# A mixture-of-experts gather that reads a reordered copy of its rows, in a four-part fused kernel

## The chip, the cores and the metric

The kernel runs on one core of a Trainium2 chip as one launch. The metric is the device time of one execution in microseconds, as the median over runs. TensorE (PE, with its weight loads shown apart as PEld), VectorE (DVE), ScalarE (ACT), GpSimd (POOL) and SyncE (SP) are the engines named below. SP does nothing here but issue weight loads, and GpSimd issues the small loads.

## The reference

Two layers of a transformer block (four kinds of attention, a cross attention over a memory, and a mixture of experts) are followed by four layers of a second block (pooling, neighbourhood attention, convolution, pooling) on 256 rows of width 1024, all in float32. What matters here is the mixture of experts of the first block:

```python
def hierarchical_moe(x, w_group, b_group, w_expert, b_expert, w_gate, w_up, w_down):
    ...
    hid = jax.nn.silu(jnp.einsum('sd,edf->sef', xs, w_gate)) * jnp.einsum('sd,edf->sef', xs, w_up)
    return jnp.einsum('sef,efd->sd', hid * gates[:, :, None], w_down)
```

Each of the 256 rows picks one of 8 groups of experts and two of the four experts in it, so each expert sees only the few rows that chose it. The hidden width of an expert is 256, and an expert's three matrices are 1 MB each.

## The kernel before

The stage `moe` (from line 1477) runs once in each of the two layers. It takes the 32 experts as 8 quads `q` of four. The router (line 1307) gives every row its rank within each expert. Each expert has 32 slots in a pass, so a quad has 128 slots. A one-hot matrix `disp` (line 1388, or a piece of the `y` tiles in the first quad and in extra passes) says which row goes into which slot.

`gather` multiplies: the stationary operand (`lhsT`, loaded as weights) is a 128-column piece of `x`, the moving operand is the one-hot matrix of 128 columns, and the result is the chosen rows, transposed, for one eighth of the width. There are 8 pieces and two blocks of 128 rows, so 16 matmuls for a gather. A float32 matmul appears in the trace as two records of each kind, so a gather is 32 PE records. The pieces are `self.x[tb][:, k0 + j::8]`: every eighth column, since the expert weights are loaded with `(p k)` rows.

After the gather come the gate and up products with 32 columns of weights (`gate_up`, `ps<-w,xg`), the down products (`down`, `ps<-w,y`) and the scatter back into four accumulators (`acc<-y,ct`). The order on PE is: gate and up of quad q, gather of quad q+1, the small transposes of `combine_mats` and `down_in`, down of quad q. In between run pieces of other work that the stage carries along, marked `pl`: the memory's keys and values in layer 0, and the pooling of the second block's context in layer 1.

An expert with more than 32 rows needs more passes. `mores[q]` is the number of passes of a quad, held in a register of every engine. Behind `tc.If(more > 1)` stands a first extra pass, inside it behind `tc.If(more > 2)` a second, unrolled too, and inside that behind `tc.If(more > 3)` a loop for the rest. This stands twice for each quad, in the up part (lines 1533 to 1541) and in the down part (lines 1584 to 1591). All engines run through these branches; the hint of `mark_branch_hint_location` is given for PE alone. A loop of this kind is compiled with a close in which every engine waits for the work and the loads issued ahead of it.

The weights come through rings of 1 MB buffers, filled by SP in the order of use. A load is issued when its buffer is free, so SP waits for PE.

Ahead of the router's scores stands the affine step of the layer norm (`ln_affine`, lines 1098 to 1105), on the four halves of `x`: two on GpSimd, two on DVE, a multiplication and an addition each. At the end of the stage four operations on DVE (line 1608) add the accumulators to the scaled `x`, half by half.

Of the kernel before, what the change touches and what calls it, by code (L numbers as in the profile page):

```python
# [14 lines left out]
OP = mybir.AluOpType  # L15
AX = mybir.AxisListType

P = 128
# [5 lines left out]
ALPHA = 4.0 ** 0.25  # L24
# [111 lines left out]
class Net:  # L136
# [958 lines left out]

        self.flow.spawn(gen(), 0)

    def ln_affine(self, rows, eng=None):

        for tb in range(2):  # L1100
            for nh in range(2):
                e = eng[2 * tb + nh] if eng else self.nc.gpsimd
                x = self.x[tb][:, nh * 512:nh * 512 + 512]
                e.tensor_tensor(x, x, rows[0][nh], OP.mult)
                e.tensor_tensor(x, x, rows[1][nh], OP.add)

    def trans_bank(self, xs, j):

# [197 lines left out]
    def router(self, l, wr, rb):  # L1306

        nc = self.nc
        xf = [self.M2("xf32") for _ in range(4)]
        yield 0, 4.0  # L1310
        for j in range(4):
            self.affine_t(xf[j], self.trans_bank(self.halves(self.x), j), j,
                          lambda k: self.col("ln_mem_g", 8 * l + k), lambda k: self.col("ln_mem_b", 8 * l + k))
            yield 0.6, 0
        self.ln_affine(self.rows, (nc.gpsimd, nc.gpsimd, nc.vector, nc.vector))
        yield 0, 0.8
        p = self.ps()
        for tb in range(2):
# [25 lines left out]
        p = self.ps()  # L1344
# [47 lines left out]
    def gather(self, d, xg):  # L1392

        res = []
        dv = d.rearrange("p t e s -> p t (e s)")
        for k0 in range(0, 8, 4):
            p = self.ps()
            for j in range(4):
                for tb in range(2):
                    self.mm(p[:, j * P:(j + 1) * P], self.x[tb][:, k0 + j::8], dv[:, tb, :], tb == 0 and j == 0, tb == 1)  # L1400
            t = xg[k0 // 4].rearrange("p (k s) -> p k s", k=4)
            if k0:
                self.nc.vector.tensor_copy(xg[1], p)  # L1403
            else:
                self.nc.scalar.copy(xg[0], p)
            res += [t[:, j, :] for j in range(4)]
        return res
# [68 lines left out]
    def moe(self, l):  # L1476
        nc, tc = self.nc, self.tc
# [7 lines left out]
        hx = self.e("hx", [P, EXTRA * 256])  # L1485
# [3 lines left out]
        h, h2 = self.places()  # L1489
# [11 lines left out]
        def between(n):  # L1501

            if l == 0:
                if n in MEM_AT:
                    self._ahead()
                    yield from self.piece(side[0])
            elif n in (3, 6, 7):
                yield from self.piece(side[0])
            elif 10 <= n <= 21:
                self._ahead()  # L1510
                yield from self.piece(side[1])

        for q in range(8):
            if q == 1 and l == 0:
                prep = self.flow.spawn(self.band(), 0)
            wg = [self.raw("E", "expert_w_gate", l, 4 * q + j, 8) for j in range(4)]
            wu = [self.raw("E", "expert_w_up", l, 4 * q + j, 8) for j in range(4)]
            gv, uv = [w for w, _ in wg], [w for w, _ in wu]
            more = mores[q]
            rk = self.s("rk", [P, 2, 4], bufs=1)  # L1520
            if q:
                h, h2 = self.places()

            def extra_up(out):
                nc.vector.tensor_scalar(rk, rk, -32.0, None, OP.add)
                self.gate_up(self.gather(self.dispatch(rk, onehot(h2)), [self.y(0), self.y(1)]), gv, uv, out)

            gates = gates or rest()
            now, d0 = comb, d
            if q < 7:  # L1530
                d = self.dispatch(rank[:, :, 4 * q + 4:4 * q + 8])
            self.gate_up(xg, gv, uv, h)
            with tc.If(more > 1, label=f"up{l}_{q}"):  # L1533
                nc.vector.tensor_copy(rk, rank[:, :, 4 * q:4 * q + 4])
                extra_up(hx[:, 0:256])
                with tc.If(more > 2):
                    extra_up(hx[:, 256:512])
                    with tc.If(more > 3):
                        with tc.For_i(3, more) as i:
                            extra_up(h2)  # L1540
                            nc.vector.tensor_copy(hx[:, self.at(i)], h2)
            tc.mark_branch_hint_location(f"down{l}_{q}", more > 1, pe)
            for _, i in wg + wu:
                self.used(i)
            if q == 3:
                self.far.close()
                if l:
                    self.near.close()
                    assert self.plan is None or not self.live_p
                self.other(split=SPLITS, more=MORE[l])  # L1550
                if l:
                    self.perm, self.capp = self.near.enter_context(self.tc.tile_pool(name="late", bufs=LATE, reuse_waits="tile", side="right")), LATE
                self.keep, self.stage = True, 2 * l + 1
                self.n_split = SPLITS
                self.pump()
                main.lane = "ps"
            yield 8.5, 0
            yield from between(3 * q)
            if q < 7:
                xg = self.gather(d, xt)  # L1560
                now = now or self.combine_mats(flat(d0), gates[:, :, 0, :])
                comb = self.combine_mats(flat(d), gates[:, :, q + 1, :])
                ht = self.down_in(h)
                yield 5.0, 0 if q > 2 else 3.0
                yield from between(3 * q + 1)
            else:
                ht = self.down_in(h)
            if q == 7 and not l:
                self.adas.append(self.flow.spawn(self.ada(1), 2, 6.0))
            gq = gates[:, :, q, :]  # L1570
            wd = [self.raw("E", "expert_w_down", l, 4 * q + j, 2) for j in range(4)]
            dv = [w for w, _ in wd]

            def extra_down(h, src=None):
                dx, h2 = self.places()
                if h is None:
                    h = h2
                    nc.vector.tensor_copy(h, src)
                nc.vector.tensor_scalar(rk, rk, -32.0, None, OP.add)
                d2 = self.dispatch(rk, onehot(dx))  # L1580
                self.down(self.down_in(h), dv, *self.combine_mats(flat(d2), gq, "x"))

            def extras():
                with tc.If(more > 1, label=f"down{l}_{q}"):
                    nc.vector.tensor_copy(rk, rank[:, :, 4 * q:4 * q + 4])
                    extra_down(hx[:, 0:256])
                    with tc.If(more > 2):
                        extra_down(hx[:, 256:512])
                        with tc.If(more > 3):
                            with tc.For_i(3, more) as i:  # L1590
                                extra_down(None, hx[:, self.at(i)])

            self.down(ht, dv, *now, q == 0)
            extras()
            if q < 7:
                tc.mark_branch_hint_location(f"up{l}_{q + 1}", mores[q + 1] > 1, pe)
            if q == 7:
                nc.scalar.preload_act_table_set("natural_log_exp_and_others")
            for _, i in wd:
                self.used(i)  # L1600
            if q == 7:
                self._ahead()
            if q == 7:
                st = [self.s("bn", [P, 2, 6], bufs=2) for _ in range(2)]
                for half in range(2):
                    for tb in range(2):
                        x = self.x[tb][:, half * 512:half * 512 + 512]
                        nc.vector.scalar_tensor_tensor(x, x, ALPHA, self.acc[tb][half], OP.mult, OP.add)
                        self.bn_half(st, half, tb)
            yield 6.0, 0 if q > 2 else 10.0  # L1610
            yield from between(3 * q + 2)
            if q == 2 and l == 0:
                yield prep.done
# [530 lines left out]
    def layer_b(self, l):  # L2144

        with ExitStack() as ctx:
            self.phase(ctx, 6)
            self.stage = 2 * l
            self.other(ring2=RING2)
            self.exp = ctx.enter_context(self.tc.tile_pool(name="exp", bufs=1, reuse_waits="tile"))  # L2150
            self.y = lambda i, dt=F32: self.e(f"y{i}", [P, 512], dt)
            self.rows = [[], []]
            for i in range(4):
                t, c = self.y(i), i % 2 * 512
                self.nc.sync.dma_start(t, self.a["ln_mem" + ("_g", "_b")[i // 2]][l:l + 1, c:c + 512].to_broadcast([P, 512]))
                self.rows[i // 2].append(t)
            self.wr = self.router_weights(l)
            self.pump()
            yield from self.moe(l)

# [188 lines left out]
```

## Time and profile before

| | us |
|---|---|
| median of 3 runs | 1836.73 (1834.0 to 1844.76) |
| the profiled execution | 1837.78 |
| its span, first to last instruction | 1836.0 |
| stage `moe`, layer 0 (gather of quad 0 to the last scatter) | 306 to 602 |
| stage `moe`, layer 1 | 876 to 1250 |

The profiled execution lies 1.05 us above the median and has 1.8 us outside its span. [...] Further views read the trace of one stretch: the waits of an engine with the one that released it, the windows with busy times and granted clock, and the timeline of an engine.

### The profile page before, as it was taken

The page shows a single profiled execution, that of the slowest core. Times are in us where ns is not written, and L with a number is a line of the kernel's source. Part 1 is how long each engine was busy: PE and PEld are TensorE (multiplying, and loading weights), DVE is VectorE, ACT ScalarE, POOL GpSimd, SP SyncE. Part 2 cuts the span into 40 slices and gives each one's busy share as a digit, 9 for nine tenths or more (in the row PEclk, how much of TensorE's full clock was granted, in tenths as well). Part 3 has the DMA queues.
Part 4 walks back from the last instruction along what each step waited for, and adds up shares of the span by engine and source line. Part 5 has one row for each costly group of instructions (what it writes and reads, how often), then busy time and mean ns, then how long its engine had stood idle before and what let it go on. Part 6 is the DMA issues. An engine that isn't in the chain of part 4 may idle for free. (4 is left out here: it accounts for less than half of the span.)

```text
span 1836.0 us, 29061 instructions
## 1 busy us (share of the span) xinstructions
PE 1649.1 (90%) x11357; PEld 1297.9 (71%) x11357; DVE 918.4 (50%) x2160; ACT 701.1 (38%) x1422; POOL 165.9 (9%) x248
## 2 busy tenths in 40 slices
PE   7999997788888799988898898997998999899997
PEld 6767985556765466686656675866887886699785
DVE  5567545252112756766121243247555566576645
ACT  4654540102212355442010132234545565455543
POOL 4000201000000300031000000002001112000101
PEclk9999998899999899999899999998998999999999
DMA  8266557989957955576357497897456866385630
GB/s 306 85 204 229 187 206 302 389 327 416 364 197 310 385 164 183 184 285 255 129 223 329 168 412 301 317 364 280 139 188 135 207 97 84 121 293 171 235 111 24
DMA packets 145964, 427.29 MB, mean 233 GB/s; under 512 B 12252, under 2 KB 19652, under 8 KB 121172
## 3 DMA queue, kind: packets, MB, share of 16 engines
q1 hardware_dynamic: 140660, 411.19, 60.6%
q0 software_dynamic: 5088, 13.32, 5.3%
q8 instruction: 124, 2.03, 0.5%
q14 instruction: 92, 0.75, 0.1%
HBM read 423.43 MB, written 1.05 MB: 231 GB/s over the span
## 5 line engine op out<-in xcount | busy, mean ns | idle before, releaser
L308 DVE TENSOR_TENSOR wlo<-w,whi 128x512 fp32r<-128x512 f32 (+2 forms) x586 | 395.4, 709 | 265.0 <-ACT whi L307 262.8
L307 ACT CAST whi<-w 128x512 fp32r<-128x512 f32 (+2 forms) x592 | 341.5, 611 | 249.6 <-PE ps L366 199.1
L366 PE MATMUL ps<-xth,whi 128*128 128x256 f32 x896 | 263.9, 295 | 8.7 <-ACT whi L307 5.2
L366 PE MATMUL ps<-xth,wlo 128*128 128x256 f32 x896 | 259.3, 289 | 4.4 <-DVE wlo L308 4.4
L366 PE MATMUL ps<-xtl,whi 128*128 128x256 f32 x896 | 258.5, 289 | 0.6 <-DVE xtl L1142 0.4
L366 PE MATMUL ps<-whi,xth 128*128 128x512 f32 (+2 forms) x512 | 206.6, 404 | 4.4 <-ACT whi L307 4.0
L366 PE MATMUL ps<-wlo,xth 128*128 128x512 f32 (+2 forms) x512 | 198.8, 388 | 0.2 <-DVE wlo L308 0.2
L366 PE MATMUL ps<-whi,xtl 128*128 128x512 f32 (+2 forms) x512 | 198.6, 388 | 0.2 <-DVE xtl L1142 0.2
L366 PEld LDWEIGHTS ps<-xth,whi 128*128 128x128 f32 x896 | 176.0, 196 | 18.1 <-ACT whi L307 12.8
L366 PEld LDWEIGHTS ps<-xth,wlo 128*128 128x128 f32 x896 | 174.8, 195 | 5.2 <-DVE wlo L308 5.2
L366 PEld LDWEIGHTS ps<-xtl,whi 128*128 128x128 f32 x896 | 175.2, 196 | 3.2 <-issue 1.4
L366 PEld LDWEIGHTS ps<-whi,xth 128*128 128x128 f32 x512 | 99.0, 193 | 33.2 <-ACT whi L307 6.6
L366 PEld LDWEIGHTS ps<-whi,xtl 128*128 128x128 f32 x512 | 98.4, 192 | 20.7 <-DVE xtl L1142 0.9
L366 PEld LDWEIGHTS ps<-wlo,xth 128*128 128x128 f32 x512 | 98.9, 193 | 18.3 <-DVE wlo L308 1.3
L366 PE MATMUL ps<-disp,x 128*128 128x128 f32 x384 | 94.4, 414 | 15.7 <-PEq L1533 6.8
L366 PEld LDWEIGHTS ps<-disp,x 128*128 128x128 f32 x384 | 93.0, 336 | 19.0 <-issue 14.3
L366 PE MATMUL ps<-w,xg 128*32 128x256 f32 x1536 | 86.9, 382 | 6.1 <-issue 2.8
L366 PE MATMUL ps<-w,y 128*32 128x512 f32 (+1 forms) x784 | 80.9, 551 | 6.9 <-DVE y L1451 4.4
L366 PEld LDWEIGHTS ps<-w,xg 128*32 128x32 f32 x1536 | 52.1, 111 | 40.2 <-issue 7.3
L1142 POOL TENSOR_TENSOR xtl<-aff,xth 128x512 fp32r<-128x512 f32 x9 | 11.6, 1285 | 696.9 <-ACT xth L1141 521.5
L1403 DVE COPY xg<-ps 128x512 f32<-128x512 f32 x14 | 9.7, 692 | 118.9 <-PE ps L366 118.9
L1435 DVE TENSOR_TENSOR y<-y,ps 128x256 f32<-128x256 f32 x12 | 5.1, 421 | 112.6 <-ACTq L1533 62.9
(516 smaller groups left out, 2567.0 us busy)
## 6 DMA issues: line engine op xcount, KB each, us to landing
w<-in_expert_w_gate_dram SPq DMA_DIRECT2D x64, 1024.0 KB, 14.4
w<-in_expert_w_up_dram SPq DMA_DIRECT2D x64, 1024.0 KB, 12.6
w<-in_expert_w_down_dram SPq DMA_DIRECT2D x64, 1024.0 KB, 10.0
w<-in_ada_w_dram SPq DMA_DIRECT2D x48, 1024.0 KB, 6.1
w<-in_pool_w_in_dram SPq DMA_DIRECT2D x24, 1024.0 KB, 10.9
w<-in_na_w_in_dram SPq DMA_DIRECT2D x24, 1024.0 KB, 6.5
w<-in_w_in_dram SPq DMA_DIRECT2D x16, 1024.0 KB, 11.5
w<-in_conv_w_in_dram SPq DMA_DIRECT2D x16, 1024.0 KB, 6.0
```

The source lines that it names most:

```text
L307: self.nc.scalar.copy(hi, src)
L308: (self.nc.gpsimd if self.spare and k % 2 else self.nc.vector).tensor_tensor(lo, src, hi.bitcast(F32), OP.subtract)
L366: self.nc.tensor.matmul(out, lhsT, rhs, start=start, stop=stop, skip_group_check=True)
L1142: (nc.gpsimd if j == 2 else nc.vector).tensor_tensor(lo, fs[j - 1], hi.bitcast(F32), OP.subtract)
L1403: self.nc.vector.tensor_copy(xg[1], p)
L1435: nc.vector.tensor_tensor(h, sg, p[:, 256:512], OP.mult)
```

## The change

The addition of `ln_affine` ahead of the router writes its result to a new pair of tiles `xp`, of shape 128 x 8 x 128, in which column `8 j + k` of `x` stands at `[k, j]`. `gather` reads the 128-column piece `xp[tb][:, k0 + j, :]`, which is unbroken. At the end of the stage line 1608 reads `xp` in place of `x`, through the same reordering, and writes `x` in natural order.

In the extra code the second, unrolled pass goes, and the loop runs from 2 in place of 3, in the up part and in the down part.

The SBUF kept for the descriptors of GpSimd's DMAs is set to 8192 bytes of a partition, where it was 16384; the two new tiles take 8192 bytes.

```diff
--- before.py
+++ after.py
@@ -1095,14 +1095,18 @@
 
         self.flow.spawn(gen(), 0)
 
-    def ln_affine(self, rows, eng=None):
+    def ln_affine(self, rows, eng=None, xp=None):
 
         for tb in range(2):
             for nh in range(2):
                 e = eng[2 * tb + nh] if eng else self.nc.gpsimd
                 x = self.x[tb][:, nh * 512:nh * 512 + 512]
                 e.tensor_tensor(x, x, rows[0][nh], OP.mult)
-                e.tensor_tensor(x, x, rows[1][nh], OP.add)
+                o, b = x, rows[1][nh]
+                if xp:
+                    o = xp[tb].rearrange("p k j -> p j k")[:, nh * 64:nh * 64 + 64, :]
+                    x, b = (v.rearrange("p (j k) -> p j k", k=8) for v in (x, b))
+                e.tensor_tensor(o, x, b, OP.add)
 
     def trans_bank(self, xs, j):
 
@@ -1312,7 +1316,7 @@
             self.affine_t(xf[j], self.trans_bank(self.halves(self.x), j), j,
                           lambda k: self.col("ln_mem_g", 8 * l + k), lambda k: self.col("ln_mem_b", 8 * l + k))
             yield 0.6, 0
-        self.ln_affine(self.rows, (nc.gpsimd, nc.gpsimd, nc.vector, nc.vector))
+        self.ln_affine(self.rows, (nc.gpsimd, nc.gpsimd, nc.vector, nc.vector), self.xp)
         yield 0, 0.8
         p = self.ps()
         for tb in range(2):
@@ -1397,7 +1401,7 @@
             p = self.ps()
             for j in range(4):
                 for tb in range(2):
-                    self.mm(p[:, j * P:(j + 1) * P], self.x[tb][:, k0 + j::8], dv[:, tb, :], tb == 0 and j == 0, tb == 1)
+                    self.mm(p[:, j * P:(j + 1) * P], self.xp[tb][:, k0 + j, :], dv[:, tb, :], tb == 0 and j == 0, tb == 1)
             t = xg[k0 // 4].rearrange("p (k s) -> p k s", k=4)
             if k0:
                 self.nc.vector.tensor_copy(xg[1], p)
@@ -1534,11 +1538,9 @@
                 nc.vector.tensor_copy(rk, rank[:, :, 4 * q:4 * q + 4])
                 extra_up(hx[:, 0:256])
                 with tc.If(more > 2):
-                    extra_up(hx[:, 256:512])
-                    with tc.If(more > 3):
-                        with tc.For_i(3, more) as i:
-                            extra_up(h2)
-                            nc.vector.tensor_copy(hx[:, self.at(i)], h2)
+                    with tc.For_i(2, more) as i:
+                        extra_up(h2)
+                        nc.vector.tensor_copy(hx[:, self.at(i)], h2)
             tc.mark_branch_hint_location(f"down{l}_{q}", more > 1, pe)
             for _, i in wg + wu:
                 self.used(i)
@@ -1585,10 +1587,8 @@
                     nc.vector.tensor_copy(rk, rank[:, :, 4 * q:4 * q + 4])
                     extra_down(hx[:, 0:256])
                     with tc.If(more > 2):
-                        extra_down(hx[:, 256:512])
-                        with tc.If(more > 3):
-                            with tc.For_i(3, more) as i:
-                                extra_down(None, hx[:, self.at(i)])
+                        with tc.For_i(2, more) as i:
+                            extra_down(None, hx[:, self.at(i)])
 
             self.down(ht, dv, *now, q == 0)
             extras()
@@ -1604,8 +1604,10 @@
                 st = [self.s("bn", [P, 2, 6], bufs=2) for _ in range(2)]
                 for half in range(2):
                     for tb in range(2):
-                        x = self.x[tb][:, half * 512:half * 512 + 512]
-                        nc.vector.scalar_tensor_tensor(x, x, ALPHA, self.acc[tb][half], OP.mult, OP.add)
+                        x = self.x[tb][:, half * 512:half * 512 + 512].rearrange("p (j k) -> p j k", k=8)
+                        xp = self.xp[tb].rearrange("p k j -> p j k")[:, half * 64:half * 64 + 64, :]
+                        acc = self.acc[tb][half].rearrange("p (j k) -> p j k", k=8)
+                        nc.vector.scalar_tensor_tensor(x, xp, ALPHA, acc, OP.mult, OP.add)
                         self.bn_half(st, half, tb)
             yield 6.0, 0 if q > 2 else 10.0
             yield from between(3 * q + 2)
@@ -2155,6 +2157,7 @@
                 self.nc.sync.dma_start(t, self.a["ln_mem" + ("_g", "_b")[i // 2]][l:l + 1, c:c + 512].to_broadcast([P, 512]))
                 self.rows[i // 2].append(t)
             self.wr = self.router_weights(l)
+            self.xp = [self.e(f"xp{tb}", [P, 8, P]) for tb in range(2)]
             self.pump()
             yield from self.moe(l)
 
@@ -2333,7 +2336,7 @@
     from concourse import mybir as _mybir
     from concourse.bass_utils import run_bass_kernel_spmd as _run
 
-    nc = _bacc.Bacc("TRN2", target_bir_lowering=False, num_devices=1)
+    nc = _bacc.Bacc("TRN2", target_bir_lowering=False, num_devices=1, dynamic_dma_scratch_size=8192)
     arrays, args = {}, {}
     for name in _INS:
         v = _np.ascontiguousarray(inputs[name])
```

## Rows read from the trace of the kernel before

**Rows 1.** Busy us of each engine over the span, with share and instructions.

```profile
PE 1649.1 (90%) x11357; PEld 1297.9 (71%) x11357; DVE 918.4 (50%) x2160; ACT 701.1 (38%) x1422; POOL 165.9 (9%) x248
```

**Rows 2.** Waits of PE, 296 to 605 us: waiter <- releaser: us, times, longest.

```profile
PE pl L366 <- PEq L1533: 4.8, 1, 4.8
...
PE ps L366 <- DMA w<-in_expert_w_down_dram: 0.3, 1, 0.3
```

**Rows 3.** Tile x, weight loads: ns min/median/max of one, first and last start.

```profile
L366 PEld LDWEIGHTS ps<-disp,x x384: 312/337/342, 323.5 to 1207.1; 128*128 128x128 f32 x192
```

**Rows 4.** Timeline of PE, two gathers: start, us, instruction, count [idle ahead].

```profile
438.87 7.89 PE L366 MATMUL ps<-disp,x 128*128 128x128 f32 x32 [2.28 <-PEq L1533]
...
966.95 7.89 PE L366 MATMUL ps<-disp,x 128*128 128x128 f32 x32 [1.24 <-DVEq L1533]
```

**Rows 5.** Timeline of PE: unbroken 128x128 weights; 256, 40 and 120-136 columns.

```profile
253.26 3.61 PE L366 MATMUL ps<-xkt,xqt 128*128 128x256 f32 x16
...
291.27 3.69 PE L366 MATMUL ps<-wr,xf 128*128 128x40 f32 x32
...
1084.73 2.88 PE L366 MATMUL pl<-band,pu 128*128 128x136 f32 x24 [0.42 <-PEq L1533]
```

**Rows 6.** Tile rk: what each extra pass runs on DVE.

```profile
L1525 DVE TENSOR_SCALAR rk<-rk x4: 165/172/172, 527.9 to 994.8; 128x8 f32<-128x8 f32 x4
...
L1534 DVE COPY rk<-rank x3: 164/165/165, 527.7 to 994.6; 128x8 f32<-128x8 f32 x3
```

**Rows 7.** Windows over gathers: length, busy PE PEld DVE ACT POOL, PEclk, DMA, GB/s.

```profile
306.10:313.80 7.70, 7.66 (x32) 7.70 (x32) 0.00 (x0) 0.58 (x1) 0.54 (x2) 0.63 1.01 412
...
438.90:446.60 7.70, 7.70 (x33) 7.70 (x34) 0.00 (x0) 0.58 (x1) 0.00 (x0) 0.78 1.02 417
...
966.90:974.60 7.70, 7.65 (x32) 7.68 (x33) 0.00 (x0) 0.59 (x1) 0.00 (x0) 1.00 1.02 419
```

**Rows 8.** Windows over like side work: after an idle of 3.85 us, and later.

```profile
479.10:482.50 3.40, 3.01 (x14) 3.02 (x15) 1.51 (x3) 0.64 (x2) 0.00 (x0) 0.50 0.92 347
485.10:488.50 3.40, 3.40 (x31) 3.40 (x30) 0.10 (x1) 0.00 (x0) 0.00 (x0) 1.00 0.99 395
```

**Rows 9.** Windows over parts of the stage in layers 0 and 1.

```profile
330.00:530.00 200.00, 169.09 (x1490) 126.26 (x1490) 64.44 (x176) 35.13 (x64) 2.96 (x8) 0.93 0.92 369
...
874.00:1246.00 372.00, 330.00 (x2768) 241.90 (x2772) 107.28 (x262) 84.18 (x162) 8.86 (x14) 0.94 0.71 281
890.00:920.00 30.00, 25.50 (x248) 20.94 (x240) 3.55 (x11) 3.22 (x5) 0.00 (x0) 0.89 0.00 1
948.00:960.00 12.00, 10.66 (x84) 5.52 (x86) 3.89 (x11) 2.31 (x4) 0.00 (x0) 1.00 0.09 19
```

**Rows 10.** Issues of line 246, the weight loads: min/median/max.

```profile
DMA to landing us min/median/max: 3.7/9.8/20.6
```

**Rows 11.** Branches of lines 1533 and 1584 on PE: ns min/median/max.

```profile
L1533 PEldq COMPARE_BRANCH  x16: 89/1960/5817, 319.6 to 1232.3; - x16
...
L1584 PEldq COMPARE_BRANCH  x16: 76/430/1358, 338.9 to 1249.8; - x16
```

**Rows 12.** Timeline of all engines: the affine step ahead of the router.

```profile
294.90 1.59 POOL L1105 TENSOR_TENSOR x<-x,y 128x512 f32<-128x512 f32 x1
...
297.08 0.69 DVE L1105 TENSOR_TENSOR x<-x,y 128x512 f32<-128x512 f32 x1
...
298.29 0.23 DVE L1322 TENSOR_TENSOR lg<-ps,rb 128x80 f32<-128x80 f32 x1
```

**Rows 13.** Line 1608, then a strided and an unbroken DVE reduction.

```profile
L1608 DVE SCALAR_TENSOR_TENSOR x<-x,acc x8: 668/670/689, 603.3 to 1257.4; 128x512 f32<-128x512 f32 x8
...
L689 DVE TENSOR_REDUCE gsel<-ident x1: 242/242/242, 87.7 to 87.7; 128x12 f32<-128x48 f32 x1
...
L1333 DVE TENSOR_REDUCE r_st<-r_el x2: 220/220/220, 300.1 to 870.5; 128x2 f32<-128x64 f32 x2
```

**Rows 14.** GpSimd's DMA issues with the most pieces: KB, us to landing.

```profile
nab<-in_na_rpb_dram POOLq DMA_DIRECT2D x32, 96.0 KB, 5.9
```

## Prediction

> **What bounds the kernel now.** I read the busy times first: PE works 90% of the span, no other engine over 50% [rows 1]. That alone says little about one stage, so I read the waits of PE in `moe` of layer 0 next. The reader is to see what is missing there: of all waits only 0.3 us are for an expert's weights, and the longest ones come from branches [rows 2]. So PE sets the pace of the stage, and time taken from PE is time won, until the weights become late. How near they are shows in the windows: between 330 and 530 us the DMA engines are busy 0.92 of the time and move 369 GB/s, where a stretch with the DMA full moves 417 [rows 7, 9]. In layer 1 they are busy 0.71 of the time [rows 9].
>
> Then I asked what a gather costs. It is 32 records of PE in 7.89 us, with the last one about 0.4 us long, so one record every 7.49 / 31 = 0.241 us [rows 4]. The weight load of a record takes 337 ns [rows 3]. The same spacing is found where the granted clock averages 1.00 and where it averages 0.78 [rows 4, 7]. A spacing that ignores the clock is not set by the array; what is left is the reading of weights whose elements lie 32 bytes apart. Matmuls with unbroken 128x128 float32 weights are the control: 32 records with 40 columns take 3.69 us, about 0.11 each, and 24 records with up to 136 columns take 2.88 us, less 0.26 for the last one 2.62 / 23 = 0.114 [rows 5].
>
> **The change, part by part.** *The gather.* There are 16 gathers for the quads and 4 for extra passes (line 1525 runs 4 times, in 3 quads) [rows 6], 20 in all. At a spacing of 0.113 one gather wins 32 x (0.241 - 0.113) = 4.1 us. Nearly all of it lies on PE's path, since PE goes on with the transposes of `combine_mats`, and the copies of the gathered rows are needed only by the next quad. In an extra pass they are needed at once, but there the first half's copy runs beside the second half's matmuls.
>
> The clock cuts this. [...] The two first gathers give 2.6, the other 18 up to 18 x 4.1 = 74, together 77 us.
>
> Of these 18, 12 have a mean clock of 0.78 and one of 0.63, like the one at 438.9 us; five have 1.00, like that at 966.9 [rows 7]. [...] The one at 438.87 stands behind 2.28 us of idle time, the one at 966.95 behind 1.24 [rows 4]: I read the fall as the joint work of the idle time and of a gather in which the array waits for its weights, as side work shows a fall behind 3.85 us of idle time with no gather [rows 8]. A denser gather should save those with little idle time ahead and leave some of the others. I take 5 falls, -8 us, between 0 and 13 of them (0 and -22).
>
> *The weights.* In layer 0 between 330 and 530 us the stretch can shrink by the DMA's free share alone, 200 x (1 - 369/417) = 23 us, and six gathers begin there, 25 us. Layer 1 has room. I take -3, at worst -15, if loads bunch up behind the branches.
>
> *The vector work.* Per layer six operations on DVE and four on GpSimd now step by 512 bytes on one side. On GpSimd the last addition ends at 296.5, and the first gather starts at 306.1 [rows 12, 7]: an addition of 1.59 us could double, twice, and be hidden. On DVE it isn't: the additions stand straight ahead of the router's first step at 298.3 [rows 12], and line 1608 at the end of the stage holds up the next one. The nearest row is a reduction of 48 elements read 128 bytes apart, 242 ns, against 220 ns for 64 unbroken ones [rows 13]. If none of the 220 grows with the elements, the step adds 22 ns to 48 elements, 0.23 us to 512; if all of it does, 77 ns, 0.8 us to 512. Twelve such operations in two layers make -3 to -10 us, and 0 if the 12 sums of that row, not its step, cost the time. I take -3, since a part of each operation is fixed.
>
> [...]
>
> *The loop.* One quad, the first of layer 1, has two extra passes (three copies of the rank for four passes [rows 6]). Its second now runs as one turn of the loop, up and down. A turn adds a copy of 256 columns (0.4 us, by the 0.67 of line 1608 for 512 [rows 13]), the setting up, and the close, in which each engine waits for all others and for every load issued before. At the up part no load is in flight (DMA share 0.00 from 890 to 920), at the down part hardly any (0.09) [rows 9]. So I price it at a copy, a dozen waits of the sequencer and a jump like the median of line 1533, 1.96 us [rows 11]: 3 us each, -6. From below, the inner `If` goes, +1; from above, two jumps at 5.8 us [rows 11] in place of one in each part, -20 in all.
>
> *The shorter code.* Nothing of the removed pass ran in the other 15 quads, so what can change is the jump over it. PE takes 1.96 us in the median for that of line 1533, 0.43 for that of line 1584 [rows 11]; the hint doesn't hide the first. Over two bodies in place of three both remain jumps. The down body of PE is the short one, and there the target may be at hand already: +2, between -3 and +8.
>
> *The DMA scratch.* GpSimd's issues with the most pieces carry 96 KB, two at a time, and land in 5.9 us [rows 14]. Nothing queues behind them that would fill half the space. I take 0; if each of the 32 were issued late by half its landing, up to -20 would lie in the attention of the second block.
>
> Sum: 77 - 8 - 3 - 3 - 6 + 2 = 59 us. The profiled execution of 1837.8 becomes 1779; the median lies 1.05 below it, so 1778.
>
> **The rivals.** *The load and the columns don't overlap.* Weights of 128x128 loaded while the previous ones work would then cost 0.11 for the load plus 0.108 for 128 columns (half of (3.61 - 0.38) / 15 = 0.216 for 256 [rows 5]), 0.22 a record: a gain of 0.02 x 640 = 13 us, less 10 for vectors, weights, loop and jumps: 1836.7 - 3 = 1834. Against it: 256 columns take 0.216 with their load, not 0.32, and the 24 records with 0.114 have both [rows 5]. [...]
>
> *The weights become the bound.* Layer 0 then wins about half of the free 23 us and the two gathers outside that stretch with what they have, some 15 of 33 us: 1778 + 18 = 1796. For it: 0.92 busy. Against it: PE waits for a weight for 0.3 us in all, and SP's next loads wait for buffers that PE frees, so a faster PE also starts them earlier.
>
> *Slower: the loop.* Its close stops all engines until the loads have landed, and the ring starts again from empty. A load lands up to 20.6 us after its issue [rows 10]; with two jumps of 5.8 us, a refill of the median 9.8 us and a copy that makes 42 us, and two such turns 84, of which the forecast holds 6: 1778 + 78 = 1856. It decides from 37 us a turn (59 + 6 + 9 over two), that is only if the loads ahead of it are still queued to the last. Against it stand the DMA shares of 0.00 and 0.09 [rows 9].
>
> *The change doesn't do what it says:* the spacing stays at 0.241, because it isn't the step of the weights. Then the costs of vectors, loop and jumps remain, 1836.7 + 7 = 1844. Against it speak [rows 5], where little else differs.
>
> **How the numbers follow.** The forecast, PE's path shorter by about 59 us, has 0.80. The weights as the bound have 0.12; the load that doesn't overlap 0.04; the loop 0.02; the stride without effect 0.02. The range takes the likeliest with its bounds: at the best end all falls of the clock go, vectors and weights cost nothing and the jumps win, 77 + 4 = 81, 1756; at the worst end 13 falls remain, the weights cost 10 and the loop 10, 77 - 22 - 10 - 10 - 4 = 31, 1806, which takes in the weights' rival. A change of 0.5%, 9 us, is about what this measurement tells from none. Faster by more: 0.80 + 0.12 = 0.92; within: the load that doesn't overlap and the stride without effect, 0.06; slower: the loop, 0.02.
>
> **What would show it.** The gather's records would stand about 0.11 us apart, 0.21 where the clock is at its lower level, with weight loads far under 337 ns; the stage would shrink by some 27 us in layer 0 and 32 in layer 1, and the rest of the kernel would keep its length. Fewer gathers would show a mean clock under 1. PE's waits for weights would stay under 5 us; if they reach 15 in layer 0, the weights' rival is right. Lines 1105 and 1608 on DVE would take 0.2 us more, at most 0.8. In quad 0 of layer 1 the close of the loop would stand as 2 to 4 us of idle PE, up and down. The forecast is wrong if the spacing stays over 0.2 at the upper clock, or if the idle time of PE grows by what the gathers win.

## The result, and the profile after

The changed kernel takes 1784.45 us in the median, against 1840.74 for the kernel before over all its runs of that comparison. The ratio is 0.9701, interval 0.9658 to 0.9743, which is 55 us of 1837; 59 were forecast. On another chip it was 0.9706 (0.9675 to 0.9736). The profiled execution has a span of 1782.4 us, 53.6 less than before. PE stays the busiest engine, and its busy time fell from 1649.1 [rows 1] to 1585.1:

```profile
PE 1585.1 (89%) x11357; PEld 1230.3 (69%) x11357; DVE 925.4 (52%) x2162; ACT 701.8 (39%) x1422; POOL 166.2 (9%) x248
```

Two gathers on the timeline of PE after the change answer to [rows 4]. The third line is the start of one at a granted clock of 0.50 (380.06 to 383.60 us), its first 16 records.

```profile
433.26 3.81 PE L366 MATMUL ps<-disp,xp 128*128 128x128 f32 x32 [1.13 <-DVEq L1537]
...
403.34 3.81 PE L366 MATMUL ps<-disp,xp 128*128 128x128 f32 x32 [1.30 <-DVEq L1537]
...
380.06 3.75 PE L366 MATMUL ps<-disp,xp 128*128 128x128 f32 x16 [3.26 <-DVEq L1537]
```

32 records take 3.81 us in place of 7.89, the last one being 0.28 long: (3.81 - 0.28) / 31 = 0.114 us a record, as the control of [rows 5]. The weight loads of tile `xp` (min/median/max in ns) fell from the 337 ns of [rows 3] to 192:

```profile
L366 PEld LDWEIGHTS ps<-disp,xp x384: 186/192/338, 324.0 to 1155.7; 128*128 128x128 f32 x192
```

Where the 53.6 us lie, from the starts on PE's timelines of both kernels:

| stretch, us | before | after | difference |
|---|---|---|---|
| start to the first gather of layer 0 | 306.1 | 307.4 | +1.3 |
| stage of layer 0, first gather to last scatter | 296.6 | 270.4 | -26.2 |
| to the first gather of layer 1 | 273.6 | 283.5 | +9.8 |
| stage of layer 1 | 374.0 | 337.1 | -36.9 |
| to the end | 585.6 | 584.1 | -1.5 |

So the two stages win 63 us, and about 10 are given back outside them. The windows over the two stages and the stretch between them (length, busy PE, PEld, DVE, ACT, POOL, granted clock of TensorE as a share of full speed, DMA share, GB/s), first of the kernel before:

```profile
306.14:602.76 296.62, 253.99 (x2176) 185.96 (x2176) 81.53 (x220) 52.26 (x96) 3.50 (x10) 0.92 0.84 333
876.39:1250.39 374.00, 334.14 (x2788) 243.54 (x2788) 107.61 (x258) 86.70 (x165) 8.86 (x14) 0.94 0.72 282
...
608.00:862.00 254.00, 232.71 (x1321) 174.27 (x1321) 165.68 (x414) 117.90 (x278) 35.45 (x34) 0.95 0.66 229
```

and of the changed one:

```profile
307.39:577.77 270.38, 225.09 (x2175) 153.75 (x2176) 81.14 (x220) 52.07 (x96) 3.51 (x10) 0.94 0.90 363
861.22:1198.31 337.09, 295.13 (x2787) 205.20 (x2788) 108.32 (x260) 86.60 (x165) 8.87 (x14) 0.97 0.78 308
584.00:846.00 262.00, 235.31 (x1310) 177.37 (x1311) 166.56 (x414) 118.03 (x278) 34.25 (x34) 0.93 0.63 221
```

The idle time of PE, length less busy time, is to be read first: 42.6 and 39.9 us before, 45.3 and 42.0 after. It hardly moved, while the DMA share rose from 0.84 to 0.90 in layer 0. What the gathers won came off the stages with little loss. The third line shows the other side: the stretch between the stages holds nearly the same matmuls (1321 and 1310 records), but its granted clock fell from 0.95 to 0.93 and it takes 8 us more.

The waits of PE for weights, in layer 0 (three lines) and in layer 1 (two), where [rows 2] had 0.3 us in layer 0:

```profile
PE ps L366 <- DMA w<-in_expert_w_up_dram: 2.4, 2, 1.9
PE ps L366 <- DMA w<-in_expert_w_down_dram: 0.6, 1, 0.6
PE pl L366 <- DMA w<-in_expert_w_gate_dram: 0.5, 1, 0.5
...
PE ps L366 <- DMA w<-in_expert_w_up_dram: 1.2, 2, 0.8
PE ps L366 <- DMA w<-in_expert_w_down_dram: 0.8, 1, 0.8
```

The vector work, first as DVE's timeline ahead of the router has it, then the residual line at the end of the stages, now line 1610 (ns min/median/max):

```profile
297.37 0.67 DVE L1104 TENSOR_TENSOR x<-x,y 128x512 f32<-128x512 f32 x1
298.08 1.03 DVE L1109 TENSOR_TENSOR xp<-x,y 128x512 f32<-128x512 f32 x1
...
299.54 0.23 DVE L1326 TENSOR_TENSOR lg<-ps,rb 128x80 f32<-128x80 f32 x1
```

```profile
L1610 DVE SCALAR_TENSOR_TENSOR x<-xp,acc x8: 1005/1047/1093, 578.3 to 1206.4; 128x512 f32<-128x512 f32 x8
```

The addition grew from 0.69 to 1.03 us [rows 12], the residual operation from 0.67 [rows 13] to 1.05.

### The profile page after: what moved, and what is told of

Its sections match the earlier page's. It is cut to its first block, busy times and chain, and to the rows that moved or that the text cites. A ratio compares the mean times of both kernels' runs of the same rounds, so it can differ in the third digit from the quotient of the medians.

```text
span 1782.4 us, 29217 instructions
## 1 busy us (share of the span) xinstructions
PE 1585.1 (89%) x11357; PEld 1230.3 (69%) x11357; DVE 925.4 (52%) x2162; ACT 701.8 (39%) x1422; POOL 166.2 (9%) x248
## 3 DMA queue, kind: packets, MB, share of 16 engines
HBM read 423.43 MB, written 1.05 MB: 238 GB/s over the span
## 5 line engine op out<-in xcount | busy, mean ns | idle before, releaser
L366 PE MATMUL ps<-xth,whi 128*128 128x256 f32 x896 | 262.4, 293 | 7.2 <-DVE x L1610 3.8
L366 PE MATMUL ps<-w,xg 128*32 128x256 f32 x1536 | 90.8, 385 | 10.4 <-issue 3.7
L366 PE MATMUL ps<-disp,xp 128*128 128x128 f32 x384 | 52.5, 301 | 16.2 <-DVEq L1537 6.8
L366 PEld LDWEIGHTS ps<-disp,xp 128*128 128x128 f32 x384 | 50.7, 215 | 20.0 <-issue 13.3
L366 PEld LDWEIGHTS ps<-w,y 128*32 128x32 f32 x784 | 25.2, 113 | 50.6 <-issue 36.0
```

The costliest lines, as they stand in the source:

```text
L366: self.nc.tensor.matmul(out, lhsT, rhs, start=start, stop=stop, skip_group_check=True)
```

## The experiments

**The step of the weights, or the fresh copy.** The copy stays, in natural order, and is read with the old step:

```diff
-                    self.mm(p[...], self.xp[tb][:, k0 + j, :], dv[:, tb, :], ...)
+                    self.mm(p[...], self.xp[tb].rearrange("p k j -> p (k j)")[:, k0 + j::8], dv[:, tb, :], ...)
```

(`ln_affine` and the residual line use `xp` unbroken in this kernel.)

> The changed kernel with one thing put back: the copy holds the columns in natural order, and the gather reads every eighth of it, 32 bytes apart. The other tile, the loop, the shorter code and the scratch stay as changed. Theory (the step of the weights costs the time): records 0.241 us apart as in the kernel before, some 65 us back, less 3 us because the vector work is unbroken again: 1784 + 62 = 1846, between 1832 and 1850, no faster than the kernel before by over 0.5%. Rival (what helps is that the gather reads another tile than the one that the vector work uses): spacing 0.113, time 1781.

Measured: ratio 0.996 (0.9938 to 0.9982). The loads of `xp` and a gather on PE's timeline:

```profile
L366 PEld LDWEIGHTS ps<-disp,xp x384: 312/336/342, 326.7 to 1203.3; 128*128 128x128 f32 x192
```

```profile
438.24 7.89 PE L366 MATMUL ps<-disp,xp 128*128 128x128 f32 x32 [1.14 <-DVEq L1536]
```

The old spacing is back, to the hundredth, in a tile that is otherwise the new one. The step is the cause and the copy is not. The kernel is still 7 us faster than before, though, which the gather cannot have done. Against the changed kernel's 0.9701 the step gives 48 us back, where 62 were expected. The two stages of the profiles differ by 58 us (667 and 608, first gather to last scatter); the changed kernel loses 9 us between the stages, where it takes 283 us and this one 274.

**The two parts alone.** First the reordered copy with both passes unrolled as before:

```diff
                 with tc.If(more > 2):
-                    with tc.For_i(2, more) as i:
-                        extra_up(h2)
-                        nc.vector.tensor_copy(hx[:, self.at(i)], h2)
+                    extra_up(hx[:, 256:512])
+                    with tc.If(more > 3):
+                        ...
```

> The reordered copy alone, with both extra passes unrolled as before. Prediction's step (loop -6, jumps +2): 4 us faster than the changed kernel, 1780. Rival (the shorter code saves jumps, the loop costs next to nothing: idle time of PE in the stage of layer 1 fell from 47.9 to 44.4 us): 3 to 4 us slower than the changed kernel, 1788. If within 3 us of 1784, neither part matters.

Measured: 0.9773 (0.9738 to 0.9808), 42 us of 1842; the changed kernel has 0.9701 and 0.9706, some 12 us more. Then the other way round, the kernel before with nothing but the diff of the extra code:

> The kernel before with the loop from 2 and one unrolled pass, nothing else. Prediction's step: 4 us slower than the kernel before (ratio 1.002). Rival (jumps saved, loop nearly free): 3 to 4 us faster (ratio 0.998). The gather's spacing stays at 0.241 in both. A loop that stops everything for 37 us a turn would give a ratio of 1.04. In the first quad of layer 1 the second extra pass of the up part is followed by 1 to 4 us more of idle PE.

Measured: 0.9951 (0.9928 to 0.9973), 9 us faster, between 5 and 13. The two ratios multiply to 0.9725, near the whole change. So the shorter code is worth 9 to 12 us, and the prediction had it at a loss of 4. The windows over the two stages of the kernel with the loop alone:

```profile
306.13:597.57 291.44, 253.56 (x2175) 185.68 (x2176) 81.15 (x220) 52.10 (x96) 3.51 (x10) 0.93 0.85 339
874.14:1248.49 374.35, 335.65 (x2787) 243.70 (x2788) 108.34 (x260) 86.75 (x165) 8.87 (x14) 0.95 0.71 281
```

PE's idle time in them is 37.9 and 38.7 us, against 42.6 and 39.9; two profiles of the changed kernel differ by 2 us in layer 0. Part of the difference has one name: the inner branch, from the end of the first extra pass over the code of the further ones (line 1536 in both kernels). Its time on PE's sequencer, ns min/median/max, before:

```profile
L1536 PEldq COMPARE_BRANCH  x5: 75/197/3404, 542.0 to 1012.5; - x5
```

and with the loop alone:

```profile
L1536 PEldq COMPARE_BRANCH  x5: 75/187/580, 539.0 to 1008.5; - x5
```

In the two quads with exactly one extra pass it took 3.31 and 3.40 us, and now takes 0.42 and 0.58. In the changed kernel (there line 1540) the two are 0.80 and 3.22, where the reordered copy alone, with both passes unrolled, has 3.73 and 3.84. So a shorter jump isn't always a cheap one, and the jump accounts for 5.7 us of the 9 in one comparison and for 3.6 of some 12 in the other. The values are of two kinds, 0.4 to 0.8 and above 3 us, and no view here shows what gives a jump the one or the other. What is left I could not name in the profile; it is within the intervals.

**How the price grows with the step.** Pieces 0 to 3 with a step of two elements, 4 to 7 with four:

```diff
+    def piece_of(self, xp, k):
+        f = xp.rearrange("p k j -> p (k j)")
+        if k < 4:
+            return f[:, 256 * (k // 2) + k % 2:256 * (k // 2) + 256:2]
+        return f[:, 512 + k % 4::4]
...
```

> The copy holds pieces 0 to 3 with a step of two elements (8 bytes) and pieces 4 to 7 with a step of four (16 bytes), so that half of each gather has each. Theory 1 (each column that begins in a new 16 bytes pays the full price): the half with four elements at 0.241, the half with two between 0.113 and 0.18. Theory 2 (the price grows in proportion to the step, 0.241 at 32 bytes): 16 bytes 0.12, 8 bytes hidden behind the columns at 0.113. Theory 3 (any broken step has the price): 0.241 in both halves. Times by the spacing: 1784 plus 20 gathers x 16 records x the excess over 0.113, that is 41 us for one half at 0.241, plus some 4 us for the vector work in three pieces: 1829, 1789, 1870.

Measured: 0.979 (0.9748 to 0.9831). A gather on PE's timeline, its first half, and the rest with two records of the first half; then the loads of `xp`:

```profile
433.21 2.12 PE L366 MATMUL ps<-disp,xp 128*128 128x128 f32 x16 [1.13 <-DVEq L1554]
...
434.94 4.13 PE L366 MATMUL ps<-disp,xp 128*128 128x128 f32 x18
```

```profile
L366 PEld LDWEIGHTS ps<-disp,xp x384: 193/311/333, 325.0 to 1171.2; 128*128 128x128 f32 x192
```

From start to start the records with 8 bytes stand 117 to 119 ns apart, those with 16 bytes 232 to 234. That is theory 1: 16 bytes cost nearly as much as 32 (241), and 8 bytes cost next to nothing behind 128 columns (114). Why the price comes between 8 and 16 bytes, no run shows. The time came out below the forecast of 1829: the records account for 31 us more than in the changed kernel, the ratio for 16. PE's idle time is lower there (280.35 - 240.30 = 40.1 us in layer 0) than in the changed kernel (45.3), and by 3 us in layer 1, so 8 us of the loss fall into waits and the two stages are 23.5 us longer. Another 6 us come from the stretch between the stages, 276.6 us in place of 283.1: this profile has the short form of the softmax stretch that is told of below.

**A loop for every extra pass.** The loop runs from 1, without an unrolled pass:

```diff
-                extra_up(hx[:, 0:256])
-                with tc.If(more > 2):
-                    with tc.For_i(2, more) as i:
+                with tc.For_i(1, more) as i:
...
```

The down part has the same.

> The changed kernel with no unrolled extra pass: the loop runs from 1, so the three quads with extra passes make four turns, up and down, where the changed kernel makes one. Two of the quads are new to the loop: quad 6 of layer 0 (DMA share 0.25 from 510 to 528 us in the changed kernel) and quad 2 of layer 1 (DMA share 1.00 from 960 to 978). Theory (a turn costs a copy and 1 to 2 us of idle PE, up and down, whatever is in flight): four turns in place of one, 3 x 3 = 9 us slower, less up to 4 us for the inner jumps that go: 1784 + 5 = 1789. Rival (the close stops all engines until the loads in flight have landed, up to 20 us, and the ring starts from empty): quad 2 of layer 1 loses 15 to 40 us in its up part, quad 0 as little as before: 1805 or more.

Measured: 0.9911 (0.988 to 0.9941), 38 us slower than the changed kernel. The theory of a cheap turn fell, and the loss didn't lie where the rival had put it. So the loop was split by quads, with the same edit behind `l == 1 and q == 0`, and behind `l == 0 or q`:

> The changed kernel with the loop from 1 in the first quad of layer 1 alone: two turns there, up and down, in place of one unrolled pass and one turn; the DMA is idle in that stretch. [...] Rival (the loss of the kernel with all passes in the loop came from the quads with loads in flight, and from the later ones): within 5 us of the changed kernel.

> The other half: the loop from 1 in quad 6 of layer 0 and in quad 2 of layer 1, one turn each, and the first quad of layer 1 as in the changed kernel. Theory (a turn is dear only behind another turn): 2 to 4 us a quad, 1788. Rival (the closes with loads in flight are dear): 1800 or more, with idle PE of 10 us or more in one of the two quads.

Measured: 0.9871 (0.9844 to 0.9897) for the first, 30 us over the changed kernel's 0.9706 on that chip, where the rival had it within 5, and 0.9765 (0.9734 to 0.9796) for the second, 11 us over it. The dear one is the quad with two turns. The windows over its down part, and over the second quad, first of the changed kernel in its second profile:

```profile
904.00:940.70 36.70, 32.51 (x311) 19.04 (x311) 9.55 (x29) 6.59 (x12) 2.17 (x4) 1.00 0.78 311
940.70:962.10 21.40, 17.95 (x209) 11.97 (x209) 4.42 (x13) 2.72 (x5) 0.00 (x0) 1.00 1.01 417
```

and of the kernel with two turns:

```profile
899.80:946.00 46.20, 35.17 (x310) 19.80 (x310) 9.78 (x30) 6.58 (x12) 2.16 (x4) 0.93 0.69 273
946.00:974.40 28.40, 22.05 (x209) 15.44 (x209) 4.34 (x13) 2.71 (x5) 0.00 (x0) 0.82 1.01 417
```

The same matmuls take 9.5 and 7.0 us more, partly as idle time (11.0 and 6.4 in place of 4.2 and 3.5) and partly at a clock of 0.93 and 0.82 in place of 1.00. What stands between two turns on PE's timeline:

```profile
919.02 0.97 PE L366 MATMUL acc<-y,ctx 128*128 128x512 f32 x3 [0.29 <-DVE y L1469]
923.84 0.70 PE L369 MATMUL ps<-ident,y 128*128 128x128 f32 x2 [3.85 <-DVE y L1585]
...
925.57 3.64 PE L366 MATMUL ps<-w,y 128*32 128x512 f32 x16
```

3.85 us of idle time, and behind it the down products at half speed, 3.64 us in place of 1.92.

The expectation took the DMA to be idle here. It is in the turns of the up part (share 0.00 from 868.5 to 899.8 us), but not in the first extra pass of the down part. The first window is the first of the two turns, the second the single turn of the changed kernel (second profile), which stands behind an unrolled pass; the last line is a wait of SP in the close between the two turns:

```profile
912.50:920.00 7.50, 7.20 (x48) 3.30 (x48) 2.59 (x8) 1.75 (x3) 0.00 (x0) 1.00 1.01 422
...
923.80:931.30 7.50, 7.19 (x48) 3.33 (x48) 2.63 (x8) 1.75 (x3) 0.00 (x0) 1.00 0.18 75
...
SPq L1594 <- DMA w<-in_expert_w_gate_dram: 2.3, 1, 2.3
```

The DMA share is 1.01 in the one and 0.18 in the other. PE's last product of the first turn ends at 920.0 us, the close waits until 922.3 for a load of gate weights to land, and the next turn begins at 923.5. So 2.3 of the 3.85 us are the rival's price, a close with loads in flight, and the rest is the turn itself. In the changed kernel the last load lands at 924.7 us, early in the single turn, and PE works on that turn until 931.3, so no load holds up its close.

With the up part (48.0 us in place of 43.5) that makes 21 of the 34 us by which the stage of layer 1 is longer; the other 13 lie in later quads, at a clock of 0.94 in place of 0.99 and with longer jumps, and I could not settle why the loop should bring those. In the kernel with single turns the rival shows again: PE waits 9.0 us for weights in layer 1, the longest 6.84 us ahead of the gather that follows the up part's loop in quad 2. This gather reads no weights of an expert. SP waits in the close, load by load, until 983.6 us, and PE goes on at 984.35, so it is the close with loads in flight that holds PE.

```profile
984.35 5.24 PE L366 MATMUL ps<-disp,xp 128*128 128x128 f32 x32 [6.84 <-DMA w<-in_expert_w_up_dram]
```

**Where PE stops being the bound.** In layer 0 half of the gather is left out:

```diff
+                last = 0 if self.stage < 2 else 1
-                for tb in range(2):
+                for tb in range(last + 1):
...
```

> The changed kernel, in layer 0 with the gather's matmuls for the first 128 rows alone, 16 records in place of 32; the second 128 rows are left out there. The routing of layer 1 is then another one, so only the stage of layer 0 is read (270.4 us in the changed kernel, with 3.4 us of waits for weights). PE gets another 9 x 16 x 0.113 = 16 us or more. Theory (PE still sets the pace): the stage shrinks by 12 us or more, waits for weights under 8 us. Rival (the weights are now the bound in layer 0, DMA share 0.93 from 330 to 530 us): it shrinks by under 6 us, waits for weights grow by 10 us or more.

Measured for the stage of layer 0: 264.0 us, 6.4 less than in the changed kernel, while the gathers' own time, first to last record, fell from 38.5 to 20.8. The window:

```profile
308.20:572.16 263.96, 213.07 (x2031) 140.17 (x2032) 80.97 (x220) 52.11 (x96) 3.52 (x10) 0.93 0.93 374
```

Neither theory holds as it was put. Waits for weights are 6.1 us, 2.7 more, not 10; but of 17.7 us only 6.4 are won. Idle time is 50.9 us, 5.6 more (2.7 of it weights, the rest mostly longer jumps). PE's busy time fell by only 12.0 us, at a clock of 0.93 in place of 0.94: the other records took longer. Layer 0 is near the end of what a faster PE gives.

**The residual in natural order.** GpSimd copies `xp` back into `x` in the fifth quad, and the residual line reads `x`:

```diff
+            if q == 4:
+                for tb in range(2):
+                    for k in range(0, 8, 4):
+                        nc.gpsimd.tensor_copy(self.x[tb].rearrange("p (j k) -> p k j", k=8)[:, k:k + 4, :], self.xp[tb][:, k:k + 4, :])
```

> The changed kernel with the residual step at the end of the stage reading x in natural order again; in the fifth quad GpSimd writes x back from the reordered copy (four operations of 512 elements a layer, beside PE's work). Theory (the strided reading costs the 0.38 us of each of the eight operations, on the path): eight operations at 0.67 us, 3 us faster than the changed kernel, 1781. Rival (GpSimd's operations hold up VectorE while they run, or the path runs elsewhere): 1784 to 1788.

Measured: 0.9672 (0.962 to 0.9724). It ran once more, on the same chip as the changed kernel:

> The version in which GpSimd writes x back in natural order, on the same chip as the changed kernel. The four operations ahead of the norm take 4.6 us in place of 6.1 in each layer: 3 us faster than the changed kernel, less than the comparison can tell.

> The changed kernel once more, beside the next one. If the low clock from 710 to 727 us in the first profile was chance, the part between the two stages takes 254 to 257 us in place of 261.6, and the span is some 5 us shorter; if it belongs to the change, it stands there again.

Measured there: 0.9693 (0.9672 to 0.9714), and 0.9706 (0.9675 to 0.9736) for the changed kernel. The residual line is back at its old length,

```profile
L1612 DVE SCALAR_TENSOR_TENSOR x<-x,acc x8: 670/670/686, 576.3 to 1201.0; 128x512 f32<-128x512 f32 x8
```

0.38 us less each, 3 us in all, and no row shows a cost; the comparison cannot tell the two kernels apart.

The second profile of the changed kernel has a span of 1777.9 us. From the end of the residual line to the router's products it takes 262.4 us again (261.6 in the first). By the expectation that speaks against chance. The softmax part of that stretch, where the rows differ most, is this in the changed kernel's second profile:

```profile
685.90:720.90 35.00, 34.37 (x170) 21.37 (x170) 22.27 (x79) 18.51 (x64) 0.00 (x0) 0.83 0.40 139
```

and in the two profiles of the kernel with the residual in natural order, one and the same program, the first

```profile
679.50:709.90 30.40, 29.76 (x170) 19.29 (x170) 21.40 (x77) 17.79 (x61) 0.00 (x0) 0.98 0.47 162
```

and the second

```profile
682.70:717.70 35.00, 34.37 (x170) 21.35 (x170) 22.28 (x79) 18.51 (x64) 0.00 (x0) 0.83 0.41 140
```

The same code takes 30.4 us at a clock of 0.98 or 35.0 at 0.83. So which it is, is chance at least in part. But the three kernels with 32-byte weights all had the short one (the kernel before 30.1 us), and of ten profiles with the reordered copy six took 34.8 to 35.2 us. Whether the change makes the long one likelier stays open.

## Why the prediction was right, and where it was not

The mechanism, the direction and the total were right. The total of 59 us, measured 55, came out so near by luck, because two terms were off to opposite sides: the gather with its costs won less than forecast, the loop and the jumps more.

**The gather, 77 less 8: right.** At a granted clock of 1.00 a gather took 3.53 us from first to last record in place of 7.48, 4.0 won where 4.1 was put. The 2.6 us put for the two first gathers and the 8 for five falls were the author's estimates, which no run shows as they were put. What a lower clock does to the spacing stands in [rows 8]: 14 records in 3.01 us at 0.50 are 0.215 us each, 31 in 3.40 at 1.00 are 0.110. In place of the estimates the runs showed this: the first gathers of the layers take 5.10 and 6.31 us at mean clocks of 0.69 and 0.56, 3.5 us less than the 7.48 each before. Of the other 18, the forecast left five with a fall of the clock; the first profile has five (at 347, 380, 878, 976 and 1009 us, mean clocks 0.54, 0.56, 0.72, 0.69 and 0.69), the second four. They cost 9.8 us over the full-speed time, 8 were put. From first to last record all twenty sum to 148.8 us before and 84.6 after, without the one gap inside the third gather (1.9 and 3.6 us): 64 won, 69 forecast.

That a gather that waits for its weights helps the clock to fall, which was read from two rows, has the counts on its side. Gathers with a mean clock below 1: 15, 13 and 12 of 20 in the three kernels with 32-byte weights (before, the strided copy, the loop alone); 7, 6 and 4 in the changed kernel's two profiles and the gather alone. The windows over the stages rose with it, 0.92 to 0.94 and 0.94 to 0.97. But the kernel with two steps, in which half of each gather waits for its weights, has only 5. So the counts agree with the reading and do not show it.

**What the gathers win stays won: half right.** This is the step that failed, in size. For the gather with weights and vector work the terms gave 77 - 8 - 3 - 3 = 63 us; alone it measured 42 (35 to 48). In its profile the records win 66 us. PE's idle time in the two stages takes 12 back, of which 9 are waits for weights (9.7 in place of 0.3); the vector work takes 4. The span of that profile is 48 us shorter, so another 2 us are not placed; its execution was the fastest of four, 5 us below their median, and the ratio gives 42. The weights were put at 3 us and at worst 15; they took 9 here and 5 in the whole change. The view that was misread is the DMA share: it was read as 23 us of room in 200, as if waits could begin only when the room was used up. They begin before that (the 9.7 us stand at a DMA share of 0.90 in layer 0 and 0.77 in layer 1), and the half gather shows how far it has gone.

**The vector work, 3 us: right in sum, for another reason.** The residual line costs 0.38 us more on eight operations, 3.0 us, as the two-ended bound of 0.2 to 0.8 allowed. The affine step's additions grow on DVE, by 0.34 us. In layer 0 of the first profile that costs nothing on the path: the multiplication between them fell from 1.74 us to 0.67, when GpSimd's last operation of that step no longer ran beside it, and from the first product of the router to its first step on DVE it is 6.80 us where it was 7.02. In layer 1 this cover is missing: the multiplication takes 1.72 us and the stretch 7.51 where it was 7.01, and the second profile has 6.95 and 7.53. So the step costs between nothing and 0.5 us a layer. The forecast counted four operations with the step on GpSimd in a layer; there are two, the additions, which changes no term.

**The loop, 6 us, and the jumps, +2: wrong in sign.** Together they were put at a loss of 4; measured alone they gain 9 (5 to 13). The loop itself was priced too high: in the up part PE idles 2.07 us for the copy of the result where it idled 1.2 before, in the down part 1.1 in place of 0.7, some 1.5 us in all where 6 was put. The term with the wrong sign is the jump. The prediction counted one inner `If` less in one quad, 1 us. What it passed over is that the inner branch is also jumped in the two quads with a single extra pass, at 3.3 and 3.4 us; the rows of that branch would have shown it (line 1536, 75 to 3404 ns), but [rows 11] have lines 1533 and 1584 alone. Even so the jump names no more than 5.7 us of the gain. The outer jump did not change, as forecast: 1.97 us in the median after 1.96 [rows 11].

**The slower rival.** It was held off by the DMA shares of 0.00 and 0.09 [rows 9], and in the changed kernel that was right: its turn in the down part has 0.18, and the last load lands 6.6 us before PE is done with it. But this holds for the second extra pass alone. Where the first one is a turn too, the share is 1.01 and its close waits 2.3 us for a load, and the close of a single turn in the up part of another quad holds PE for 6.84 us until the loads have landed. So the rival's mechanism is real, at far less than its 42 us a turn. The kernel with two turns lost 30 us: by idle time between the turns, of which that wait is a part, by the lower clock behind it (0.93 and 0.82 in place of 1.00), and by 13 us in later quads that stay unexplained. The change was cheap since its only turn comes when the loads have all but landed.

**The other rivals.** The load that doesn't overlap with the columns: 0.114 us a record excludes it. The stride without effect: the strided copy excludes it. The weights as the bound were forecast to leave 1796; they took 5 us in the whole change, and the half gather says that they would take more of the next gain.

**The scratch, 0: not told apart from nothing.** The strided copy with the halved scratch and the loop has 0.996, the loop alone 0.9951. That bounds copy and scratch together to some 5 us either way; the scratch was not tried alone.

**The rest keeps its length: wrong by about 10 us.** Three are the residual line, which the forecast had. Up to one is the affine step. Some 5 are the softmax stretch, 35.2 us at a clock of 0.83 in place of 30.1 at 0.99, which no step of the prediction could have held.

## What to carry to other kernels

Read the weight spacing of every float32 matmul against an unbroken control on the same timeline: here a spacing that ignored the granted clock (0.241 us a record at 1.00 and at 0.78) went with weights that are read with a step of 32 bytes, and a copy in the reader's order cost some 0.35 us more per operation of 512 elements, where the matmuls paid 4 us a gather. Count each branch of a nest in every quad that takes any part of it, not only in the quad that runs the deepest body. Look up the DMA share in each pass that a loop is to take over, not in the last alone. Expect part of what is taken from a stage that PE bounds to come back as waits for weights and elsewhere (66 us of records became 48 of span with the gather alone), and more of the next cut (6.4 of 17.7 us were won with half of the gather left out).

## What the runs showed of the hardware that was not expected

- Weights with a step of 8 bytes load at nearly full pace (118 ns a record, where unbroken weights take 114), 16 bytes cost 233 and 32 bytes 241: the price comes between 8 and 16 bytes and hardly grows behind that.
- An addition on DVE that writes 512 elements with a step of 512 bytes takes 1.03 us where it took 0.69, and one that reads so 1.05 where it took 0.67. On GpSimd the same write took 1.27 us at its shortest, where the unbroken one took 1.26.
- The turn of a loop costs a few us of idle time, part of it for loads in flight (2.3 of 3.85 us between two turns, 6.84 us once behind a single turn), but the work behind it may run at half speed: the down products there took 3.64 us in place of 1.92, in a window with a mean clock of 0.93 in place of 1.00.
- The softmax stretch of one and the same program ran at a mean clock of 0.98 in one profile and 0.83 in another, 30.4 or 35.0 us.
